# Eight places for the next pair's tokens, combined in product order; h loaded ahead of w_out

## The chip, the core and the metric

The kernel runs on one core of a Trainium2 chip. The engines of that core are PE (matrix multiplication, with PEld for its weight loads), DVE (vector operations), ACT (scalar operations and copies), POOL and SP. Each engine takes its instructions in the order of the program; SP issues the DMA transfers between the memory of the chip and the core's SBUF. The metric is the time of one execution on the device in microseconds (us), as a median over runs.

## The reference, cut

One layer of a decoder trunk on 4096 tokens of width 1024: an input projection to ten streams, five small mixers on them, a gate, an output projection and a layer norm.

```
def hybrid_mixer(x, mem, w_in, ...):
    proj = x @ w_in                                   # 4096 x 1024 @ 1024 x 3584
    xa, ba, ca, u, v, xc, da, dg, q, gate = jnp.split(proj, SPLIT_OFFSETS, axis=-1)
    ...
    y_d = conformer_conv(da, dg, cc_dw_w, ...)        # depthwise convolution, 31 taps
    ...
    h = jnp.concatenate([y_a, y_b, y_c, y_d, y_e], axis=-1) * jax.nn.silu(gate)
    return h @ w_out                                  # 4096 x 1280 @ 1280 x 1024

def reference(x, ...):
    y = hybrid_mixer(x, mem, ...)
    return layer_norm(DEEPNORM_ALPHA * x + y, ln_g[l], ln_b[l])
```

## The kernel before

**Input projection.** Tokens go in blocks of T = 512, and two blocks make a pair; there are four pairs. For each pair `mpair` runs 14 times. One `mpair` multiplies two groups of 128 output columns with the two blocks of the pair by a scheme of the Strassen kind: seven products (PA, PT1, PT2, PB, PT3, PD, PT4, in this order) in place of eight. Each factor of a product is an fp32 value split into a high and a low part, so that a product of four steps of 128 rows is 4 x 3 = 12 matmuls (L209, L211 and L212), and an `mpair` has 84. The sums over the products are made by DVE while it reads them from PSUM (`add`, L90: tiles t, v and three tiles cc). PSUM has four banks ("mm") for the products, so that a product late in an `mpair` needs a bank that DVE has read.

**Tokens.** The right factor of product i lies in four places of SBUF, x{i}{kap}h and x{i}{kap}l: kap 0 and 1 are the first and second half of its 512 rows, h and l the high and low part. `x_prep(p)` fills all 28 places of a pair: `load` (L134) brings a quarter block of 512 KB per half, eight in all, `step` combines quarters (`sub`, L93, in place, four times per half), and `put` splits the result into its places: a cast on ACT (L86) and a subtraction on DVE (L87, tile xl). The places are those of the pair before, so a place can be written when that pair's last `mpair` has run the product that reads it. For pairs 1 to 3 `x_prep` does half 0 with its four loads and seven steps, then half 1; all eight loads use the four buffers "raw", so those of half 1 wait for buffers that half 0 has done with. The call stands in front of the last `d_in` of the pair before.

**Weights.** Their splits are made in pair 0 and stored (wd); later pairs load them back (L202) in the order of use, through five buffers "ws".

**Between the products.** `d_conv` makes 60 steps of 1.28 us on DVE for the pair before (L462, tile acc, in a buffer "big" of five), spread over the first six `mpair`s of a pair; `d_tail` then has PE transpose the result (L428). `d_in` (L449, tile din, also "big") makes the input of that convolution.

**Output projection.** After the last pair all places x.. are reused. w_out is loaded in ten tiles (buffers "raw") and split into the first 20 places, ln_g and ln_b take two more, and the last six, from x51h on, take the first split tile of h, the gated mixer outputs (`load_h(0)`, three loads, tile hraw). Then 32 row tiles follow, each of 60 matmuls (L757): k from 0 to 9, and for each k two column halves with three matmuls each. The even row tiles take h from `load_h`.

The order of instructions on an engine is the order of the code; nothing reorders them but the tile framework's own scheduling, which fixes one order per engine when the program is built.

Of the kernel before, what the change touches and what calls it, by code (L numbers as in the profile page):

```python
# [11 lines left out]
F32 = mybir.dt.float32  # L12
# [15 lines left out]
NKO = DMIX // P  # L28
# [24 lines left out]
def trunk(ctx, tc, a, out):  # L53
    nc = tc.nc
# [9 lines left out]
    def nm(s):  # L64
        uid[0] += 1
        return f"{s}_{uid[0]}"
# [5 lines left out]
    def tt(tag, dt=F32, n=None):  # L72
        cols, bufs = SLOTS[tag]
        return tp.tile([P, cols], dt, tag=tag, name=nm(n or tag), bufs=bufs)
# [7 lines left out]
    def bank(pool, tag):  # L82
        return pool.tile([P, T], F32, tag=tag, name=nm(tag))

    def split_to(hi, lo, src):
        nc.scalar.copy(out=hi, in_=src)  # L86
        nc.vector.tensor_tensor(out=lo, in0=src, in1=hi.bitcast(F32), op=ALU.subtract)  # L87
# [4 lines left out]
    def sub(dst, x, y):  # L92
        nc.vector.tensor_tensor(out=dst, in0=x, in1=y, op=ALU.subtract)  # L93
# [24 lines left out]
    def x_place(i, kap):  # L118
        return [xc.tile([P, 2, T], F32R, tag=f"x{i}{kap}{s}", name=nm(f"x{s}")) for s in "hl"]

    def x_prep(p):

        xs = [[None, None] for _ in range(7)]
        raws = {}

        def put(i, kap, src):
            xs[i][kap] = x_place(i, kap)
            split_to(*xs[i][kap], src)

        def load(kap, j, n):  # L130
            tag = "big" if p == 0 and kap == 1 else "raw"
            raw = tt(tag, n="xraw")[:, :2 * T].rearrange("p (k t) -> p k t", k=2)
            k0 = 4 * j + 2 * kap
            nc.sync.dma_start(out=raw, in_=a["xT"][:, k0:k0 + 2, (2 * p + n) * T:(2 * p + n + 1) * T])  # L134
            raws[kap, j, n] = raw

        def step(kap, i):
            b11, b12, b22, b21 = (raws.get((kap, *q)) for q in ((0, 0), (0, 1), (1, 1), (1, 0)))
            if i == PT1:
                sub(b11, b12, b11)  # L140
            elif i == PT2:
                sub(b11, b22, b11)
            elif i == PT3:
                sub(b12, b22, b12)
            elif i == PT4:
                sub(b21, b21, b11)
            put(i, kap, {PA: b11, PT1: b11, PT2: b11, PB: b21, PT3: b12, PD: b22, PT4: b21}[i])

        if p == 0:
            for q in ((0, 0), (0, 1), (1, 1), (1, 0)):  # L150
                for kap in range(2):
                    load(kap, *q)
                yield
            for i in range(7):
                for kap in range(2):
                    step(kap, i)
                yield
        else:
            for kap in range(2):
                for q in ((0, 0), (0, 1), (1, 1), (1, 0)):  # L160
                    load(kap, *q)
                for i in range(7):
                    step(kap, i)
        yield xs

# [59 lines left out]
    def mpair(xs):  # L225


        def step(ps, x, start, stop):
            ready(1)
            product(ps, ahead.pop(0), x, start, stop)  # L230
            ready(5)

        A = bank(pm, "mm")
        step(A, xs[PA], True, False)
        t = tt("st", n="t")
        nc.scalar.copy(out=t, in_=A)  # L236
        C = bank(pm, "mm")
        step(C, xs[PT1], True, True)
        B = bank(pm, "mm")
        step(B, xs[PT2], True, True)  # L240
        add(t, B, t)
        v = tt("st", n="v")
        add(v, C, t)
        step(A, xs[PB], False, True)
        B2 = bank(pm, "mm")
        step(B2, xs[PT3], True, False)
        c22 = tt("cc", n="cc")
        add(c22, B2, v)
        C2 = bank(pm, "mm")
        step(C2, xs[PD], True, True)  # L250
        c12 = tt("cc", n="cc")
        add(c12, C2, v)
        step(B2, xs[PT4], False, True)
        c21 = tt("cc", n="cc")
        add(c21, B2, t)
        return (A, c12), (c21, c22)
# [13 lines left out]
    def begin(b, key, dst):  # L270
        if b == 0:
            nc.gpsimd.memset(dst, 0.0)
        else:
            nc.gpsimd.tensor_copy(out=dst, in_=halo[key])

    xg = x_prep(0)
    first = [{}, {}]

# [360 lines left out]
    def take(gen, count):  # L639
        for _ in range(count):  # L640
            if next(gen, "end") == "end":
                return
# [21 lines left out]
    for p in range(NPAIR):  # L664
# [15 lines left out]
        for i in range(2):  # L680
            q, ge = mpair(xs)
# [8 lines left out]
        if p < NPAIR - 1:  # L690
            xs = next(x_prep(p + 1))
# [5 lines left out]
    free = [xc_tag for i in range(7) for kap in range(2) for s in "hl" for xc_tag in (f"x{i}{kap}{s}",)]  # L697

    def place(dt=F32R, n="wo"):
        return xc.tile([P, 2 * T], dt, tag=free.pop(0), name=nm(n))  # L700

    wo = []
    for k in range(NKO):
        raw = tt("raw", n="woraw")
        nc.sync.dma_start(out=raw, in_=a["w_out"][k])
        wo.append((place(), place()))
        split_to(*wo[k], raw)
    lng, lnb = place(F32, "lng"), place(F32, "lnb")
    nc.sync.dma_start(out=lng, in_=a["ln_g"])
    nc.sync.dma_start(out=lnb, in_=a["ln_b"])  # L710
    htags = free[:6]

    def load_h(u):

        def part(j):
            if u % 2 == 0 or j == 4:
                return xc.tile([P, 2 * T], F32R, tag=htags[j if u % 2 == 0 else 5], name=nm("h"))
            return tt("ws", F32R, n="h")

        src = h[u // 2][:, u % 2]  # L720
        hs = [part(j).rearrange("p (k t) -> p k t", k=4) for j in range(5)]
        for j in range(3):
            n = 4 if j < 2 else 2
            raw = tt("raw", n="hraw").rearrange("p (k t) -> p k t", k=4)[:, :n]
            nc.sync.dma_start(out=raw, in_=src[:, 4 * j:4 * j + n])
            if j < 2:
                split_to(hs[j], hs[2 + j], raw)
            else:
                split_to(hs[4][:, :2], hs[4][:, 2:], raw)
        return [(hs[k // 4][:, k % 4], hs[2 + k // 4][:, k % 4]) if k < 8 else (hs[4][:, k - 8], hs[4][:, k - 6])  # L730
                for k in range(NKO)]

    hn = load_h(0)
    for b in range(NB):
        for c in range(NC4):
            r0 = b * T + c * P
            if c % 2 == 0:
                hh = hn
            elif r0 < SEQ - P:
                if r0 == (SEQ - 2 * T) - P:  # L740
                    take(conv, 60)
                    d_tail(NPAIR - 1, accs)
                hn = load_h((r0 + P) // 256)
            take(conv, 3)
            r = [tt("cc", n="r") for _ in range(2)]
            for n in range(2):
                nc.sync.dma_start(out=r[n], in_=a["x"][r0:r0 + P, T * n:T * n + T])
            st = sp.tile([P, 2, 6], F32, tag="st2", name=nm("st2"))
            ps = [bank(pm, "mm") for _ in range(2)]
            steps = [(n, k) for k in range(NKO) for n in range(2)]  # L750
            if r0 == SEQ - P:
                steps.sort()
            for n, k in steps:
                hi, lo = hh[k]
                whi, wlo = wo[k]
                for l, ww in ((lo, whi), (hi, wlo), (hi, whi)):
                    nc.tensor.matmul(out=ps[n], lhsT=l[:, P * (c % 2):P * (c % 2) + P], rhs=ww[:, T * n:T * n + T],  # L757
                                     start=(k == 0 and l is lo), stop=(k == NKO - 1 and ww is whi and l is hi))
            for n in range(2):
                nc.vector.scalar_tensor_tensor(out=r[n], in0=r[n], scalar=ALPHA, in1=ps[n],  # L760
                                               op0=ALU.mult, op1=ALU.add)
                nc.vector.bn_stats(out=st[:, n], in_=r[n])
            mv = sp.tile([P, 2], F32, tag="mv2", name=nm("mv2"))
            nc.vector.bn_aggr(out=mv, in_=st)
            rs = sp.tile([P, 1], F32, tag="rs2", name=nm("rs2"))
            rstd_of(rs, mv[:, 1:2], 1, EPS)
            for n in range(2):
                nc.vector.scalar_tensor_tensor(out=r[n], in0=r[n], scalar=mv[:, 0:1], in1=lng[:, T * n:T * n + T],
                                               op0=ALU.subtract, op1=ALU.mult)
                nc.vector.scalar_tensor_tensor(out=r[n], in0=r[n], scalar=rs, in1=lnb[:, T * n:T * n + T],  # L770
                                               op0=ALU.mult, op1=ALU.add)
                nc.sync.dma_start(out=out[r0:r0 + P, T * n:T * n + T], in_=r[n])
# [59 lines left out]
```

## Time and profile before

| | |
|---|---|
| median of 3 runs | 1802.05 us (1799.92 to 1803.36) |
| the profiled execution | 1802.25 us |
| its span in the trace | 1800.5 us |
| busy: PE, DVE, ACT, POOL | 97%, 74%, 28%, 2% |
| mean granted clock of TensorE | 0.992 |

The profiled execution takes 1.75 us more than its span; that part lies around the span. A busy PE of 97% leaves some 45 us in which PE did nothing. [...]

### The profile page before, as it was taken

The page shows a single profiled execution, that of the slowest core. Times are in us where ns is not written, and L with a number is a line of the kernel's source. Part 1 is how long each engine was busy: PE and PEld are TensorE (multiplying, and loading weights), DVE is VectorE, ACT ScalarE, POOL GpSimd, SP SyncE. Part 2 cuts the span into 40 slices and gives each one's busy share as a digit, 9 for nine tenths or more (in the row PEclk, how much of TensorE's full clock was granted, in tenths as well). Part 3 has the DMA queues.
Part 4 walks back from the last instruction along what each step waited for, and adds up shares of the span by engine and source line. Part 5 has one row for each costly group of instructions (what it writes and reads, how often), then busy time and mean ns, then how long its engine had stood idle before and what let it go on. Part 6 is the DMA issues. An engine that isn't in the chain of part 4 may idle for free.

```text
span 1800.5 us, 21764 instructions
## 1 busy us (share of the span) xinstructions
PE 1754.9 (97%) x7912; PEld 1383.6 (77%) x7912; DVE 1336.9 (74%) x2461; ACT 507.0 (28%) x937; POOL 44.8 (2%) x87
## 2 busy tenths in 40 slices
PE   5999999999999999999999999999989999999997
PEld 4887777878877787887778788777768888888786
DVE  8678887799966539997643999766379996665665
ACT  4323644420144423013532411354141010000300
POOL 0000000000100001010000000000000000000000
PEclk9999999999999999999999999999989999999999
DMA  7767455776744467675346766544683344332621
GB/s 276 274 239 261 183 198 196 280 238 208 235 163 137 133 217 270 201 230 177 129 151 211 269 201 213 197 143 141 205 289 99 119 132 141 127 100 79 213 71 47
DMA packets 128091, 332.79 MB, mean 185 GB/s; under 512 B 14064, under 2 KB 36080, under 8 KB 127984
## 3 DMA queue, kind: packets, MB, share of 16 engines
q1 hardware_dynamic: 127984, 331.39, 54.3%
q8 instruction: 63, 1.03, 0.2%
q14 instruction: 44, 0.36, 0.1%
HBM read 238.02 MB, written 93.32 MB: 184 GB/s over the span
## 4 chain that ended last, share of the span: by engine, by line
PE 91%; DVE 5%; DMA 2%; ACT 1%; issue 1%; SPq 0%; DVEq 0%; ACTq 0%
PE mm L757 24%; PE mm L209 19%; PE mm L212 19%; PE mm L211 19%; PE ax L632 3%; PE ax L607 2%; DVE xl L87 2%; PE ax L627 2%; DMA xraw<-in_xT 1%; DVE xraw L93 1%; PE ax L577 1%; PE ax L428 1%; PE ax L485 0%; PE ax L475 0%; PE ax L487 0%
## 5 line engine op out<-in xcount | busy, mean ns | idle before, releaser
L209 PE MATMUL mm<-xl,w 128*128 128x512 f32 x1568 | 627.4, 400 | 25.9 <-DVE xl L87 20.3
L211 PE MATMUL mm<-xh,w 128*128 128x512 f32 x1568 | 624.6, 398 | 0.9 <-DVE w L87 0.9
L212 PE MATMUL mm<-xh,w 128*128 128x512 f32 x1568 | 623.2, 398 | 0.0
L757 PE MATMUL mm<-wo,h 128*128 128x512 f32 x1920 | 445.8, 394 | 7.8 <-DVE h L87 7.8
L757 PEld LDWEIGHTS mm<-wo,h 128*128 128x128 f32 x1920 | 362.6, 189 | 87.6 <-DVE h L87 8.6
L209 PEld LDWEIGHTS mm<-xl,w 128*128 128x128 f32 x1568 | 297.1, 189 | 98.6 <-DVE xl L87 24.4
L212 PEld LDWEIGHTS mm<-xh,w 128*128 128x128 f32 x1568 | 296.8, 189 | 70.6 <-issue 3.6
L211 PEld LDWEIGHTS mm<-xh,w 128*128 128x128 f32 x1568 | 297.2, 190 | 68.2 <-issue 2.4
L462 DVE SCALAR_TENSOR_TENSOR acc<-din,c,acc 128x1024 f32<-128x1024 f32 x240 | 303.8, 1279 | 0.6 <-ACT acc L459 0.2
L86 ACT CAST h<-hraw 128x1024 fp32r<-128x1024 f32 (+1 forms) x48 | 43.3, 910 | 319.8 <-PE mm L757 235.3
L90 DVE TENSOR_TENSOR cc<-mm,v 128x512 f32<-128x512 f32 x112 | 76.8, 688 | 68.8 <-PE mm L212 68.3
L760 DVE SCALAR_TENSOR_TENSOR r<-r,mm 128x512 f32<-128x512 f32 x64 | 43.5, 687 | 79.8 <-PE mm L757 79.7
L86 ACT CAST xh<-xraw 128x1024 fp32r<-128x1024 f32 x56 | 57.9, 1051 | 64.2 <-DVE xraw L93 41.5
L90 DVE TENSOR_TENSOR t<-mm,t 128x512 f32<-128x512 f32 x56 | 38.6, 689 | 49.9 <-PE mm L212 49.9
L87 DVE TENSOR_TENSOR xl<-xraw,xh 128x1024 fp32r<-128x1024 f32 x56 | 66.7, 1221 | 11.3 <-ACT xh L86 11.1
L388 ACT ACTIVATE cc<-cc 128x512 f32<-128x512 f32 x44 | 27.9, 634 | 157.2 <-DVE cc L90 157.0
L87 DVE TENSOR_TENSOR h<-hraw,h 128x1024 fp32r<-128x1024 f32 (+1 forms) x48 | 49.7, 1041 | 26.3 <-issue 13.1
L236 ACT COPY t<-mm 128x512 f32<-128x512 f32 x56 | 32.9, 587 | 128.6 <-PE mm L212 128.5
L611 DVE TENSOR_REDUCE mx<-ax 128x2 f32<-128x512 f32 x64 | 42.7, 682 | 30.2 <-PE ax L607 29.9
L90 DVE TENSOR_TENSOR cc<-mm,t 128x512 f32<-128x512 f32 x56 | 38.5, 688 | 35.6 <-PE mm L212 35.1
L615 ACT ACTIVATE e<-ax,mx 128x256 f32<-128x256 f32 x128 | 59.3, 476 | 17.1 <-DVE mx L611 16.2
L435 ACT ACTIVATE nrm<-ax,nmr,rs 128x256 f32<-128x256 f32 x64 | 30.7, 570 | 115.9 <-DVE nmr L433 115.9
(147 smaller groups left out, 1531.8 us busy)
## 6 DMA issues: line engine op xcount, KB each, us to landing
w<-wd SPq DMA_DIRECT2D x294, 512.0 KB, 3.9
wd<-w SPq DMA_DIRECT2D x98, 512.0 KB, 2.9
xraw<-in_xT SPq DMA_DIRECT2D x32, 512.0 KB, 5.5
h<-cc SPq DMA_DIRECT2D x64, 256.0 KB, 3.1
hraw<-h SPq DMA_DIRECT2D x32, 512.0 KB, 4.1
r<-in_x SPq DMA_DIRECT2D x64, 256.0 KB, 3.0
out<-r SPq DMA_DIRECT2D x64, 256.0 KB, 2.0
wraw<-in_w_in SPq DMA_DIRECT2D x22, 512.0 KB, 4.3
```

What stands on the lines that cost most here:

```text
L86: nc.scalar.copy(out=hi, in_=src)
L87: nc.vector.tensor_tensor(out=lo, in0=src, in1=hi.bitcast(F32), op=ALU.subtract)
L90: nc.vector.tensor_tensor(out=dst, in0=x, in1=y, op=ALU.add)
L209: nc.tensor.matmul(out=ps, lhsT=w[:, 0, k], rhs=xl[:, r], start=start and k == 0, stop=False, skip_group_check=True)
L211: nc.tensor.matmul(out=ps, lhsT=w[:, 1, k], rhs=xh[:, r], start=False, stop=False, skip_group_check=True)
L212: nc.tensor.matmul(out=ps, lhsT=w[:, 0, k], rhs=xh[:, r], start=False, stop=stop and k == 3, skip_group_check=True)
L462: nc.vector.scalar_tensor_tensor(out=accs[i], in0=dins[i][:, k:k + 2 * T], scalar=dww[:, i, k:k + 1], in1=accs[i], op0=ALU.mult, op1=ALU.add)
L611: nc.vector.tensor_reduce(out=mx, in_=sc[j], axis=AX.X, op=ALU.max, negate=True)
L615: nc.scalar.activation(out=e[:, c], in_=sc[j][:, c], func=AF.Exp, bias=mx[:, c:c + 1], accum_out=su[:, c:c + 1])
L632: nc.tensor.matmul(out=po[64 * j:64 * j + 64], lhsT=vm[:, mc, 64 * hd:64 * hd + 64], rhs=pT, start=(mc == 0), stop=(mc == 1))
L757: nc.tensor.matmul(out=ps[n], lhsT=l[:, P * (c % 2):P * (c % 2) + P], rhs=ww[:, T * n:T * n + T], start=(k == 0 and l is lo), stop=(k == N ...
L760: nc.vector.scalar_tensor_tensor(out=r[n], in0=r[n], scalar=ALPHA, in1=ps[n], op0=ALU.mult, op1=ALU.add)
```

## The change

Two pieces of code are changed. In `x_prep` for pairs 1 to 3 the eight loads no longer share four buffers: half 0's four and the last of half 1 are in "raw", the other three of half 1 in "big". The eight are issued ahead of all steps, in the order in which the steps first use them, and the steps go product by product, both halves of product 0, both of product 1 and so on. In the output phase the six places for h are now the first six (x00h to x10l), `load_h(0)` stands ahead of w_out, whose ten tiles take the next 20 places (x11h to x60l), and ln_g and ln_b take x61h and x61l.

```diff
@@ -128,7 +128,7 @@
             split_to(*xs[i][kap], src)
 
         def load(kap, j, n):
-            tag = "big" if p == 0 and kap == 1 else "raw"
+            tag = "big" if kap == 1 and (p == 0 or (j, n) != (1, 0)) else "raw"
             raw = tt(tag, n="xraw")[:, :2 * T].rearrange("p (k t) -> p k t", k=2)
             k0 = 4 * j + 2 * kap
             nc.sync.dma_start(out=raw, in_=a["xT"][:, k0:k0 + 2, (2 * p + n) * T:(2 * p + n + 1) * T])
@@ -156,10 +156,11 @@
                     step(kap, i)
                 yield
         else:
-            for kap in range(2):
-                for q in ((0, 0), (0, 1), (1, 1), (1, 0)):
-                    load(kap, *q)
-                for i in range(7):
+            for kap, q in ((0, (0, 1)), (0, (0, 0)), (1, (0, 0)), (1, (0, 1)), (0, (1, 1)), (1, (1, 1)), (0, (1, 0)),
+                           (1, (1, 0))):
+                load(kap, *q)
+            for i in range(7):
+                for kap in range(2):
                     step(kap, i)
         yield xs
 
@@ -699,16 +700,7 @@
     def place(dt=F32R, n="wo"):
         return xc.tile([P, 2 * T], dt, tag=free.pop(0), name=nm(n))
 
-    wo = []
-    for k in range(NKO):
-        raw = tt("raw", n="woraw")
-        nc.sync.dma_start(out=raw, in_=a["w_out"][k])
-        wo.append((place(), place()))
-        split_to(*wo[k], raw)
-    lng, lnb = place(F32, "lng"), place(F32, "lnb")
-    nc.sync.dma_start(out=lng, in_=a["ln_g"])
-    nc.sync.dma_start(out=lnb, in_=a["ln_b"])
-    htags = free[:6]
+    htags = [free.pop(0) for _ in range(6)]
 
     def load_h(u):
 
@@ -731,6 +723,15 @@
                 for k in range(NKO)]
 
     hn = load_h(0)
+    wo = []
+    for k in range(NKO):
+        raw = tt("raw", n="woraw")
+        nc.sync.dma_start(out=raw, in_=a["w_out"][k])
+        wo.append((place(), place()))
+        split_to(*wo[k], raw)
+    lng, lnb = place(F32, "lng"), place(F32, "lnb")
+    nc.sync.dma_start(out=lng, in_=a["ln_g"])
+    nc.sync.dma_start(out=lnb, in_=a["ln_b"])
     for b in range(NB):
         for c in range(NC4):
             r0 = b * T + c * P
```

SP, from the second pair to the third, before: the rows are DMA issues in their order, w<-wd weights (wd_5_183 belongs to the second pair's last `mpair`, wd_0_87 and on to the third pair's first), xraw<-in_xT tokens. Ahead of these rows the loads 5814 to 5820 of half 0 were issued while the second pair's products ran.

```order
L202 DMA w_5713<-wd_5_183 128x1024
L202 DMA w_5730<-wd_6_184 128x1024
L202 DMA w_5745<-wd_0_87 128x1024
L202 DMA w_5762<-wd_1_88 128x1024
L134 DMA xraw_5854<-in_xT 128x2x512
L202 DMA w_5777<-wd_2_89 128x1024
L202 DMA w_5794<-wd_3_90 128x1024
L134 DMA xraw_5856<-in_xT 128x2x512
L202 DMA w_5810<-wd_4_91 128x1024
L134 DMA xraw_5858<-in_xT 128x2x512
L134 DMA xraw_5860<-in_xT 128x2x512
L202 DMA w_5916<-wd_5_92 128x1024
```

SP at the same place after the change. Here the loads 5814, 5816, 5822 and 5826 were issued ahead, as they use the "raw" buffers; 5828 is the eighth load.

```order
L203 DMA w_5687<-wd_4_182 128x1024
L134 DMA xraw_5818<-in_xT 128x2x512
L203 DMA w_5713<-wd_5_183 128x1024
L134 DMA xraw_5820<-in_xT 128x2x512
L203 DMA w_5730<-wd_6_184 128x1024
L134 DMA xraw_5824<-in_xT 128x2x512
L203 DMA w_5745<-wd_0_87 128x1024
L203 DMA w_5762<-wd_1_88 128x1024
L203 DMA w_5777<-wd_2_89 128x1024
L203 DMA w_5794<-wd_3_90 128x1024
L134 DMA xraw_5828<-in_xT 128x2x512
L203 DMA w_5810<-wd_4_91 128x1024
```

Three of the four late loads moved ahead of the third pair's first weight; one load, the eighth, stands in front of its fifth weight, where before the last three stood.

DVE at the same change of pairs, before: the rows that follow the last PSUM read of the second pair (cc_5812) and the two operations din_5894. L93 combines quarters, L87 writes a low part, L462 is a step of the convolution, and the last row is the first PSUM read of the third pair.

```order
L93 TENSOR_TENSOR xraw_5854<-xraw_5856,xraw_5854 128x1024
L462 SCALAR_TENSOR_TENSOR acc_6033<-din_5691,c_222,acc_6033 128x1024
L462 SCALAR_TENSOR_TENSOR acc_6439<-din_5894,c_222,acc_6439 128x1024
L87 TENSOR_TENSOR xl_5868<-xraw_5854,xh_5867 128x1024
L93 TENSOR_TENSOR xraw_5856<-xraw_5858,xraw_5856 128x1024
L93 TENSOR_TENSOR xraw_5854<-xraw_5858,xraw_5854 128x1024
L87 TENSOR_TENSOR xl_5877<-xraw_5860,xh_5876 128x1024
L87 TENSOR_TENSOR xl_5882<-xraw_5856,xh_5881 128x1024
L87 TENSOR_TENSOR xl_5873<-xraw_5854,xh_5872 128x1024
L87 TENSOR_TENSOR xl_5886<-xraw_5858,xh_5885 128x1024
L93 TENSOR_TENSOR xraw_5860<-xraw_5860,xraw_5854 128x1024
L90 TENSOR_TENSOR t_5918<-mm_5935,t_5918 128x512
```

DVE after the change, from the row behind cc_5812 on:

```order
L93 TENSOR_TENSOR xraw_5820<-xraw_5824,xraw_5820 128x1024
L87 TENSOR_TENSOR xl_5877<-xraw_5822,xh_5876 128x1024
L87 TENSOR_TENSOR xl_5881<-xraw_5824,xh_5880 128x1024
L87 TENSOR_TENSOR xl_5873<-xraw_5820,xh_5872 128x1024
L87 TENSOR_TENSOR xl_5863<-xraw_5828,xh_5862 128x1024
L93 TENSOR_TENSOR xraw_5826<-xraw_5826,xraw_5816 128x1024
L93 TENSOR_TENSOR xraw_5828<-xraw_5828,xraw_5818 128x1024
L450 SCALAR_TENSOR_TENSOR din_5894<-th_5895,cc_5812 128x512
L87 TENSOR_TENSOR xl_5886<-xraw_5826,xh_5885 128x1024
L450 SCALAR_TENSOR_TENSOR din_5894<-cc_5796,cc_5779 128x512
L87 TENSOR_TENSOR xl_5891<-xraw_5828,xh_5890 128x1024
L90 TENSOR_TENSOR t_5918<-mm_5935,t_5918 128x512
```

Before, nine rows of xraw and xl stood between cc_5812 and t_5918, with a tenth behind it; after, nine stand there and none behind. The two convolution steps that stood among them moved behind t_5918, and the two din operations came in.

ACT at the start of the output phase, before: L86 casts the high parts of wo (w_out) and h, L447 is the tanh of `d_in`, L459 the first tap of the convolution.

```order
L86 CAST wo_11215<-woraw_11213 128x1024
L86 CAST wo_11221<-woraw_11219 128x1024
L86 CAST wo_11227<-woraw_11225 128x1024
L447 ACTIVATE cc_11152<-cc_11152 128x512
L86 CAST wo_11233<-woraw_11231 128x1024
L459 ACTIVATE acc_11258<-din_11055,c_228,c_222 128x1024
L459 ACTIVATE acc_12385<-din_11168,c_228,c_222 128x1024
L86 CAST h_11241<-hraw_11246 128x1024
L86 CAST h_11242<-hraw_11250 128x1024
L86 CAST h_11245<-hraw_11254 128x512
```

ACT after the change, around the first h cast:

```order
L448 ACTIVATE cc_11037<-cc_11037 128x512
L86 CAST h_11178<-hraw_11186 128x1024
L86 CAST h_11177<-hraw_11182 128x1024
L237 COPY t_11079<-mm_11064 128x512
L86 CAST h_11181<-hraw_11190 128x512
L86 CAST wo_11196<-woraw_11194 128x1024
L86 CAST wo_11202<-woraw_11200 128x1024
L86 CAST wo_11208<-woraw_11206 128x1024
L448 ACTIVATE th_11169<-mm_11064 128x512
L86 CAST wo_11214<-woraw_11212 128x1024
```

The three casts of h moved from behind the last of the ten wo casts to ahead of the first.

## Rows read from the trace of the kernel before

**Rows 1.** Page, busy time of each engine: us (share of the span) xinstructions.
```profile
PE 1754.9 (97%) x7912; PEld 1383.6 (77%) x7912; DVE 1336.9 (74%) x2461; ACT 507.0 (28%) x937; POOL 44.8 (2%) x87
```

**Rows 2.** Waits of PE, whole span: who for, us in total, times, longest.
```profile
PE mm L209 <- DVE xl L87: 20.3, 9, 7.6
PE mm L757 <- DVE h L87: 7.8, 2, 6.7
PE mm L209 <- DVE t L90: 4.8, 3, 3.4
```

**Rows 3.** Waits of PE in the first 45 us of the program.
```profile
PE mm L209 <- DVE xl L87: 13.3, 5, 7.6
PE mm L209 <- DVE t L90: 3.4, 1, 3.4
```

**Rows 4.** Windows, L209 only: us, PE and PEld busy (x), PEclk, DMA share, GB/s.
```profile
335.84:355.44 19.60, 11.06 (x28) 5.26 (x28) 1.00 0.78 265
355.44:381.29 25.85, 11.88 (x29) 5.64 (x28) 0.93 0.73 244
662.85:682.37 19.52, 11.05 (x28) 5.28 (x28) 1.00 0.63 214
682.37:704.92 22.55, 11.48 (x29) 5.26 (x28) 1.00 0.79 272
986.58:1006.10 19.52, 11.05 (x29) 5.28 (x28) 1.00 0.63 212
1006.10:1028.32 22.22, 11.36 (x28) 5.27 (x28) 1.00 0.79 283
1290.44:1309.96 19.52, 11.05 (x28) 5.27 (x28) 1.00 0.74 240
1309.96:1337.46 27.50, 11.14 (x28) 5.09 (x27) 0.92 0.84 297
```

**Rows 5.** Windows, L757 only: the first and second row tile of the output phase.
```profile
1337.46:1354.06 16.60, 16.59 (x61) 13.42 (x61) 0.82 0.77 256
1354.06:1367.66 13.60, 13.60 (x61) 11.27 (x60) 1.00 0.12 39
```

**Rows 6.** Windows, all of PE: the two stretches at half clock.
```profile
370.80:374.10 3.30, 3.30 (x10) 0.50 0.61 209
1333.40:1343.50 10.10, 6.04 (x14) 0.50 0.87 287
```

**Rows 7.** Chain of waits from 348 to 372 us: start, us, what.
```profile
356.05 5.56 DMA xraw<-in_xT
```

**Rows 8.** Tile xraw: ns min/median/max of its casts, subtractions and landings.
```profile
L86 ACT CAST xh<-xraw x56: 1036/1052/1059, 5.3 to 1021.9; 128x1024 fp32r<-128x1024 f32 x56
L87 DVE TENSOR_TENSOR xl<-xraw,xh x56: 1212/1222/1226, 6.3 to 1023.5; 128x1024 fp32r<-128x1024 f32 x56
...
DMA to landing us min/median/max: 3.6/5.5/9.0
```

**Rows 9.** Timeline of DVE at the second change of pairs.
```profile
683.92 0.68 DVE L90 TENSOR_TENSOR cc<-mm,t 128x512 f32<-128x512 f32 x1
...
692.67 4.62 DVE L87 TENSOR_TENSOR xl<-xraw,xh 128x1024 fp32r<-128x1024 f32 x4
...
698.35 0.69 DVE L90 TENSOR_TENSOR t<-mm,t 128x512 f32<-128x512 f32 x1
```

**Rows 10.** Windows, all of DVE: first and second change to the convolution's end.
```profile
682.37:818.01 135.64, 132.10 (x148) 1.00 0.71 233
355.44:496.17 140.73, 134.88 (x151) 0.99 0.70 231
```

**Rows 11.** Timeline of DVE and PE where the first convolution ends.
```profile
494.89 1.28 DVE L462 SCALAR_TENSOR_TENSOR acc<-din,c,acc 128x1024 f32<-128x1024 f32 x1
...
497.01 0.49 PE L428 MATMUL ax<-c,acc 128*128 128x128 f32 x3
```

**Rows 12.** Waits of SP, whole span.
```profile
SPq L134 <- DVE xl L87: 5.1, 5, 2.4
```

## The prediction

> **What bounds the kernel now.** I began with the busy times: PE does something in 97% of the span, DVE in 74% [rows 1], so PE is the bound and time can come only from the some 45 us in which it stands or runs slowly. The waits of PE say who it stood for: the low parts of the tokens (xl) 20.3 us in nine waits, the first h of the output phase 7.8 us in two, the PSUM reads of tile t 4.8 us in three [rows 2]. The start of the program holds 13.3 us of the first and 3.4 of the third [rows 3]; x_prep(0) and the first weights are not touched, so this part stays. What is left sits where the tokens of a pair give way to the next pair's, and where the output phase begins.
>
> To price these four places I read windows that hold one whole `mpair` each, the last of a pair and what follows it. Each holds 28 matmuls of L209, a third of the 84 [rows 4]. An undisturbed `mpair` takes 19.52 us, 2.79 us a product. The first `mpair` of the second pair takes 25.85 (6.25 over the 19.60 of the one before it), of the third 22.55 (3.03 over), of the fourth 22.22 (2.70 over). The last `mpair` of the fourth pair, with the wait for h that follows it, takes 27.50 (7.98 over). The first row tile of the output phase takes 16.60 us at a mean granted clock of 0.82, the second 13.60 at 1.00, so 3.00 over [rows 5]. The five excesses add up to **22.96 us**, the most that this change can give back.
>
> The clock's share lies inside that sum. PEclk was 0.50 in 370.8 to 374.1 us, after the long waits of the first change of pairs, and in 1333.4 to 1343.5 us, after the wait for h [rows 6]. Ten matmuls took 3.30 us in the first, against 10 x 0.232 = 2.32 at full clock (19.52/84 each); the second holds the slow half of the first row tile. At the second and third change the granted clock stayed at 1.00 [rows 4].
>
> **The change, part by part.** *Tokens.* Before, half 1's loads waited until half 0's splits gave back their buffers. At the first change the chain of waits runs through such a load: it took 5.56 us, and PE waited behind it [rows 7]. After the change seven loads are issued before the pair ends (the order of SP shows it), and the bytes and operations are the same: 14 casts of 1.052 us on ACT, 14 subtractions and 8 combinations of 1.222 us on DVE per pair [rows 8], 22 x 1.222 = 26.9 us of DVE. Each place still comes free as its product ends in the old pair and is needed six products later, 16.7 us on. So DVE cannot have everything done before the change: it gets free places faster (one product in 2.79 us) than it fills them (22 x 1.222/7 = 3.8 us). What matters is the order in which it catches up, and product order is the order of need.
>
> I follow the queue of DVE at a change of pairs. Let S be the time at which the new pair should start. The last PSUM read of the old pair begins at 683.92 and lasts 0.68, thus ends at S + 2.23 with S = 682.37 [rows 9, 4]. Behind it the order of DVE shows nine token operations and two din before the next read, of t. Four token operations in a row took 4.62 us [rows 9], 1.155 each; a din, half as wide, is put at the 0.68 of the cc read. That is 10.4 + 1.4 us, so t begins at S + 14.0 and ends at S + 14.7. PE wants the bank that t frees for PD, after five products, at S + 13.95: a wait of **0.7 us** at each change, 2.1 in all. Before, t began at 698.35, S + 16.0, as two convolution steps of 1.28 stood ahead of it; they have moved behind. The low part needed most urgently is PB's half 1, fifth in that queue: done at S + 2.23 + 5 x 1.155 = S + 8.0, and needed at three and a half products, S + 9.8.
>
> *The eighth load* waits for the "raw" buffer of the quarter that PT3's half 0 read; that subtraction stands two before the last PSUM read and ends near S + 0.4. With the median landing of 5.5 us [rows 8] and a cast it is ready at S + 6.95, as DVE comes to it at S + 6.9. I cost it at nothing; the price of a late landing is a rival below.
>
> *Buffers "big".* The convolution's accumulators take buffers that tokens now hold until near S + 10, so its 60 steps begin later and must still end before PE reaches their transposes. DVE was busy 134.88 of 140.73 us from the first change to the convolution's end, 132.10 of 135.64 from the second [rows 10]. At the first change the last step ended 0.84 us before PE began the transposes at 497.01 [rows 11]. With the stall taken out, PE comes there at 497.01 - 6.25 + 0.7 + 0.23 (one matmul more ahead of it in the order of PE), S + 136.25 with S = 355.44. DVE has one token operation fewer there: 133.7 busy, and with the 3.5 us of idle time of the second change it ends at S + 137.2. That is a wait of some **0.9 us**. At the other two changes the transposes stand nine matmuls (2.1 us) later than before, which covers a stall shortened by less than 2.7; I cost them at nothing.
>
> *Output phase.* The h tile's places come free with PA and PT1 of the last `mpair`, not with PD and PT4, and its loads are issued a whole pair ahead. Nothing then keeps PE from the first row tile but the last reads of PSUM, some 0.3 us by their spacing. w_out follows: k = 0 is needed at once and each further k 1.36 us later (13.60/10) [rows 5], k = 9 after 12.2 us. Its place is PT4's half 0; after that product ends, a cast and a subtraction need 2.3 us, so some 10 us cover it, and the ten splits of 1.22 us on DVE begin 16.7 us before the phase. DVE's total work is the same here too. With no wait the clock has no reason in the rows to fall, so the 3.00 us of the first row tile go as well.
>
> **The sum.** 22.96 - 2.1 - 0.9 - 0.3 = 19.7 us. From the profiled execution's 1802.25 us that gives **1782.6 us**; the median of the runs shown, 1802.05, stands 0.2 below it, too little to matter.
>
> *The clock by another road.* Without the start, xl leaves 20.3 - 13.3 = 7.0 us of waits, t 4.8 - 3.4 = 1.4, and the longest wait for h was 6.7 [rows 2, 3]: 15.1 us. The half clock adds 0.98 (3.30 - 2.32) and 3.00, so 19.1 of the 22.96 are named, and the rest are short gaps between. [...]
>
> **The rivals.** *DVE falls behind (0.12).* If each token operation takes its whole 1.222 us with one cast of 1.052 uncovered, t ends at S + 2.23 + 11.0 + 1.4 + 0.7 + 1.05 = S + 16.4, 2.4 us late at each change, 7.2 in place of 2.1: **1787.7 us**. For it: DVE has no idle time in these stretches. Against it: the measured 4.62 for four.
>
> *The convolution ends later (0.10).* If DVE finishes no sooner after the first change than before, at S + 140.73 [rows 10], PE waits 4.5 us there instead of 0.9: **1786.2 us**. For it: the later start of the accumulators.
>
> *The eighth load lands late (0.08).* At the longest landing, 9.0 us [rows 8], its low part is done at S + 11.7, PE waits 1.9 us for PB, the queue of DVE slips by 3.7 us and t costs PE 2.5 more; 4.4 per change instead of 0.7, so +11.1: **1793.7 us**. It rests on DVE taking its queue strictly in order. [...]
>
> *The clock still falls (0.03).* Waits of 0.7 us would have to do what the second and third change, with 3.03 and 2.70 us over, did not: +3.98, **1786.6 us**.
>
> *Slower than before (0.03).* SP also takes its queue in order, and the eighth load stands ahead of the new pair's fifth weight. Weights go out four products ahead, 11.2 us; with a landing like the tokens' 5.5, some 5.7 us are to spare. If SP stood there longer, each further us would cost PE one at each of three changes. It decides at 5.7 + 19.7/3 = 12.3 us: a block of 14 us would cost 24.9, and **1807.5 us** result. The longest such wait of SP was 2.4 us [rows 12].
>
> *Nothing changes (0.04).* Loads come no earlier, since another buffer binds: **1802 us**. Against it: the order of SP.
>
> My forecast has 0.60. The range of **1777 to 1794 us** takes in the first four rivals above, and at its lower end all 22.96 us with the some 2 us by which runs differ. It leaves out 0.07 above. A measurement of this kernel tells some 0.2% (3.6 us) from no change: faster 0.93, the same 0.04, slower 0.03.
>
> **What would show it right or wrong.** In the new profile the three `mpair`s after a change of pairs should take 19.5 to 20.5 us, the waits for xl should be those of the start alone, the wait for h should be gone and the granted clock should be 1.00 from 50 us on. PE should wait for t about 0.7 us at each change and about 1 us at L428 once. A wait of PE for xl at a change would mean a late eighth load; a DVE-bound t above 2 us would mean that the queue was mispriced; a weight w late would mean SP. If the first row tile still takes 16 us, the clock has another cause than the wait.

## The result and the profile after

The changed kernel takes 1783.79 us (median of 4 runs, 1783.38 to 1784.19) against 1802.68 for the kernel before in the same job: a ratio of 0.9898 (95% interval 0.9881 to 0.9915), which is 18.4 us of 1802.68; the two medians differ by 18.9. In a second job on another occasion it took 1781.54 (1780.40 to 1781.91) against 1802.17: 0.9883 (0.9870 to 0.9897). The forecast was 1782.6. The profiled execution took 1783.74 us, with a span of 1782.0.

The page's busy times, which answer to [rows 1]:

```profile
PE 1749.8 (98%) x7912; PEld 1380.8 (77%) x7912; DVE 1333.9 (75%) x2461; ACT 504.4 (28%) x937; POOL 45.6 (3%) x87
```

PE's waits over the whole span, which answer to [rows 2]:

```profile
PE mm L210 <- DVE xl L87: 13.5, 5, 7.6
PE mm L210 <- DVE t L90: 5.1, 2, 4.1
PE mm L758 <- DVE h L87: 1.3, 1, 1.3
```

Of xl's 13.5 us all lie in the first 45 us, as do 4.1 of t's 5.1. The waits for xl at the three changes of pairs are gone, and so is the long wait for h; the 1.3 us left belong to a later row tile.

Windows with the matmuls of L210 (L209 before): the first two `mpair`s of the program, then the first two of the second, third and fourth pair, then the last of the fourth. The columns are those of [rows 4]; PEclk is the clock granted to PE as a share of the full one, 1.00:

```profile
7.56:80.24 72.68, 25.30 (x56) 11.98 (x57) 0.93 0.74 268
356.52:396.82 40.30, 22.21 (x56) 10.53 (x56) 1.00 0.77 257
678.60:717.64 39.04, 22.09 (x56) 10.56 (x56) 1.00 0.73 255
999.62:1038.82 39.20, 22.12 (x57) 10.51 (x56) 1.00 0.73 247
1301.52:1321.62 20.10, 11.16 (x28) 5.09 (x27) 1.00 0.76 265
```

Two undisturbed `mpair`s take 2 x 19.52 = 39.04 us. The second pair's first two are 1.26 over, the third's nothing, the fourth's 0.16. (They are read in twos because the mark between the two falls 0.23 us earlier in the changed kernel than in the one before.) Before they were 45.37, 42.07 and 41.74 with the second `mpair` at 19.52 [rows 4], so the changes of pairs gave back 5.07, 3.03 and 2.54 us. The last `mpair` of the fourth pair takes 20.10 where it took 27.50.

The first and second row tile of the output phase, which answer to [rows 5]:

```profile
1321.62:1335.26 13.64, 13.64 (x60) 11.26 (x60) 1.00 0.97 352
1335.26:1348.87 13.61, 13.61 (x62) 11.26 (x60) 1.00 0.67 223
```

Both run at the full clock; the first gave back 2.96 us. DVE at the second change of pairs, which answers to [rows 9]:

```profile
679.19 0.69 DVE L90 TENSOR_TENSOR cc<-mm,t 128x512 f32<-128x512 f32 x1
...
680.92 4.63 DVE L87 TENSOR_TENSOR xl<-xraw,xh 128x1024 fp32r<-128x1024 f32 x4
...
691.20 0.69 DVE L90 TENSOR_TENSOR t<-mm,t 128x512 f32<-128x512 f32 x1
```

The last read of the old pair ends at 679.88, 1.28 us after the new pair's start at 678.60, and t ends at 691.89, S + 13.29. PE comes to its bank at 692.54, S + 13.94, and finds it free. The end of the first convolution, which answers to [rows 11]:

```profile
491.19 1.28 DVE L463 SCALAR_TENSOR_TENSOR acc<-din,c,acc 128x1024 f32<-128x1024 f32 x1
...
493.25 0.60 PE L429 MATMUL ax<-c,acc 128*128 128x128 f32 x4
```

The last step ends at 492.47 (S + 135.95), and PE comes to the transposes 0.78 us later without a wait.

### The profile page after: what moved, and what is told of

Its sections match the earlier page's. It is cut to its first block, busy times and chain, and to the rows that moved or that the text cites. A ratio compares the mean times of both kernels' runs of the same rounds, so it can differ in the third digit from the quotient of the medians.

```text
span 1782.0 us, 21763 instructions
## 1 busy us (share of the span) xinstructions
PE 1749.8 (98%) x7912; PEld 1380.8 (77%) x7912; DVE 1333.9 (75%) x2461; ACT 504.4 (28%) x937; POOL 45.6 (3%) x87
## 4 chain that ended last, share of the span: by engine, by line
PE 94%; DVE 3%; DMA 2%; ACT 1%; issue 0%; SPq 0%; DVEq 0%; ACTq 0%
PE mm L758 24%; PE mm L213 20%; PE mm L210 20%; PE mm L212 20%; PE ax L633 3%; PE ax L608 2%; PE ax L628 2%; DVE xl L87 1%; PE ax L578 1%; PE ax L429 1%; DMA xraw<-in_xT 1%; DVE xraw L93 1%; PE ax L486 0%; PE ax L476 0%; PE ax L488 0%
## 5 line engine op out<-in xcount | busy, mean ns | idle before, releaser
L210 PE MATMUL mm<-xl,w 128*128 128x512 f32 x1568 | 625.6, 399 | 18.8 <-DVE xl L87 13.5
L210 PEld LDWEIGHTS mm<-xl,w 128*128 128x128 f32 x1568 | 296.5, 189 | 88.8 <-DVE xl L87 15.5
L86 ACT CAST h<-hraw 128x1024 fp32r<-128x1024 f32 (+1 forms) x48 | 43.4, 909 | 311.9 <-PE mm L758 224.0
L87 DVE TENSOR_TENSOR xl<-xraw,xh 128x1024 fp32r<-128x1024 f32 x56 | 66.4, 1221 | 6.7 <-ACT xh L86 6.7
L86 ACT CAST xh<-xraw 128x1024 fp32r<-128x1024 f32 x56 | 56.9, 1047 | 46.5 <-DVE xraw L93 24.0
L87 DVE TENSOR_TENSOR h<-hraw,h 128x1024 fp32r<-128x1024 f32 (+1 forms) x48 | 50.2, 1047 | 23.3 <-ACT h L86 12.9
L633 PE MATMUL ax<-pT,c 128*64 128x512 f32 x128 | 58.9, 617 | 0.8
```

Of the source, the lines that this page charges most:

```text
L210: nc.tensor.matmul(out=ps, lhsT=w[:, 0, k], rhs=xl[:, r], start=start and k == 0, stop=False, skip_group_check=True)
L633: nc.tensor.matmul(out=po[64 * j:64 * j + 64], lhsT=vm[:, mc, 64 * hd:64 * hd + 64], rhs=pT, start=(mc == 0), stop=(mc == 1))
```

## The experiments

Each of these kernels was timed beside the kernel before. Twelve profiles beside that of before show that the first two `mpair`s of the program, which no kernel here touches, took from 70.0 to 72.7 us; differences of a microsecond between kernels are therefore read in windows, not in medians.

**The two parts apart.** Tokens alone (the x_prep part of the diff):

> Only the tokens of the change: eight places and product order; the output phase is that of before. Theory: the two parts act in different places and add up. The changed kernel gave back 5.06, 3.02 and 2.55 us at the three changes of pairs, so 10.6 us here and some 1792 us; the wait for h of 6.7 us and the slow first row tile (16.6 us) stay. Rival: part of the gain at the output phase came from tokens being ready earlier or from DVE being less late there; then this one gains more than 12 us and the other part alone less than 9.

Measured: 1791.80 us, ratio 0.9941 (0.9922 to 0.9960), 10.0 less than before. PE's waits where its output phase begins:

```profile
PE mm L758 <- DVE h L87: 6.7, 1, 6.7
```

The wait is that of before, and the first row tile took 16.20 us. The first `mpair` after each change of pairs, in this kernel and then in the changed one:

```profile
354.66:375.48 20.82, 11.17 (x28) 5.26 (x28) 1.00 0.90 311
677.51:696.80 19.29, 11.05 (x28) 5.29 (x28) 1.00 0.91 320
998.56:1017.93 19.37, 11.06 (x28) 5.26 (x28) 1.00 0.89 318
```

```profile
356.52:377.07 20.55, 11.17 (x28) 5.25 (x28) 1.00 0.89 312
678.60:697.89 19.29, 11.04 (x28) 5.28 (x28) 1.00 0.90 322
999.62:1018.99 19.37, 11.06 (x29) 5.26 (x28) 1.00 0.87 306
```

The changes of pairs are as in the changed kernel.

The output phase alone (the second and third part of the diff):

> Only the output phase of the change: h in the first six places and loaded ahead of w_out; the tokens are those of before. Theory: 7.41 + 2.95 = 10.4 us less than before, some 1792.3 us, with the three changes of pairs as before (6.2, 3.0 and 2.7 us over an undisturbed block). Rival, as for the tokens alone: less than 9 us. Beside it: in the one profile of the changed kernel the first two blocks of the program took 1.2 us longer than in the one of before. If that comes from the change of tokens it is absent here; if it is spread between executions it may show here too.

Measured: 1795.15 us (1789.66 to 1796.79), ratio 0.9953 (0.9936 to 0.9970), 6.6 less. Its first two `mpair`s after each change of pairs:

```profile
355.58:401.71 46.13, 23.11 (x56) 10.94 (x56) 0.96 0.73 244
683.55:725.55 42.00, 22.49 (x56) 10.56 (x56) 1.00 0.77 263
1007.33:1051.29 43.96, 22.65 (x57) 10.55 (x56) 1.00 0.71 252
```

Over 39.04 these are 7.09, 2.96 and 4.92 us. The last `mpair` and the first row tile (19.53 and 13.64 us) gave back all 10.9 us, but in this execution, which is the median one, the first and third change cost 3.0 us more than in the profile of before. So the parts act in separate places, as expected. The 6.6 us lie below the 9 at which the rival begins, but its other half, more than 12 us for the tokens alone, did not come (10.0), and the windows show where the rest went: to a worse draw at changes that are still open to late loads. The start of this execution took 71.3 us, so the long start of the changed kernel's first profile (72.7) isn't read from it either way; the later runs settle it as spread.

**Is it the order or the buffers?** The half order, on the changed kernel:

```diff
-            for i in range(7):
-                for kap in range(2):
+            for kap in range(2):
+                for i in range(7):
                     step(kap, i)
```

> The changed kernel with its eight places and early loads, but the steps half by half again: seven steps of half 0, then seven of half 1. Theory as the prediction put it (what matters is the order in which DVE catches up): half 1's low parts are late again, PE waits 1 to 1.5 us for xl at each change, 1787 to 1788 us. Rival: early loads are all that mattered, since the order on DVE is nearly the same for either (eight token operations and two din between the last read of a pair and t, nine before); then 1783.8 us, within 1 us, or a little less because t comes earlier.

Measured: 1781.32 us (1780.07 to 1782.71), ratio 0.9883 (0.9862 to 0.9903); no wait of PE for xl at any change. Then the one line on the buffers alone, with the loads in the old order too (output phase as changed):

```diff
-            tag = "big" if p == 0 and kap == 1 else "raw"
+            tag = "big" if kap == 1 and (p == 0 or (j, n) != (1, 0)) else "raw"
```

> The changed kernel with one line of the token part alone: the choice of buffers. The loads and the steps are in the old order again, four loads and seven steps of half 0, then of half 1. Theory after the run with the half order: the four more buffers are the whole of the token part, because the order in which DVE gets the operations is made by the scheduler from what is ready; 1781 to 1783 us, no slower than the changed kernel. Rival: the order of the loads matters, half 1's first quarters land later and PE waits for xl at each change; 1786 us or more.

> The changed kernel as it is, on the same chip as the next three, to compare with. 1783.8 us within 1 us. The first two blocks of the program took 71.5 us before, 72.7 after, and 71.0, 71.3, 72.3 and 71.0 in four other profiles; if that is spread between executions, this one lies anywhere in 70.9 to 72.8.

Measured in one job: 1781.62 us (0.9885, 0.9872 to 0.9899) and, for the changed kernel again, 1781.54. The one line's `mpair`s in twos after each change:

```profile
354.49:393.75 39.26, 22.07 (x56) 10.53 (x56) 1.00 0.75 255
676.19:715.23 39.04, 21.93 (x56) 10.55 (x56) 1.00 0.71 247
997.19:1036.39 39.20, 21.96 (x57) 10.51 (x56) 1.00 0.71 235
```

0.22, nothing and 0.16 us over (with the half order 39.27, 39.03 and 39.20 us in all): no worse than with the product order, and 0.4 to 1.0 us better at the first change. The rival of the first expectation and the theory of the second hold, and my theory of the order is refuted. The order of DVE, as the program was built, shows why: at the second and third change ten rows stand between the last read of the old pair and t in both kernels, eight of them token operations, where the changed kernel has eleven and nine. So turning the loops round moved one operation. That the tile framework puts operations in the order in which it reckons they are ready is my reading; the runs show only the orders that it built. What these two kernels win at the first change they lose in the eighth `mpair` of that pair, where PE waits to transpose a tile of another mixer, which it does not in the changed kernel:

```profile
PE ax L428 <- DVE v L404: 1.0, 1, 1.0
```

The changed kernel again came out 2.3 us below its first job, more than the 1 us expected: in its profile the first two `mpair`s took 1.3 us less, the first change 0.65, and one late row tile 0.95.

**How many buffers.** Half the dose, on the kernel with the one line: two quarters in "big", two in "raw".

```diff
-            tag = "big" if kap == 1 and (p == 0 or (j, n) != (1, 0)) else "raw"
+            tag = "big" if kap == 1 and (p == 0 or j == 0) else "raw"
```

> Half the dose: the choice of buffers alone, with two of half 1's quarters in big and two in raw, so six of the eight loads need not wait. Theory (early loads are the whole of the token part): the two late quarters are needed by the third product at the earliest; the three changes give back part of their 10.6 us, 1783 to 1788 us. Rival (each late load stalls as before, since DVE takes its queue in order): as if none were early, 1791 to 1795 us as with the output part alone.

Measured: 1782.18 us (1781.04 to 1785.97), ratio 0.9891 (0.9875 to 0.9907). The first two `mpair`s of the program, then those after each change:

```profile
8.03:78.05 70.02, 25.10 (x57) 11.73 (x57) 0.93 0.76 276
354.16:393.48 39.32, 22.05 (x56) 10.51 (x56) 1.00 0.76 266
676.54:715.62 39.08, 21.94 (x56) 10.54 (x56) 1.00 0.78 258
997.45:1036.49 39.04, 21.93 (x57) 10.55 (x56) 1.00 0.73 249
```

0.28, 0.04 and nothing over: as good as three in "big", better than my theory's 1783 to 1788. Six loads that need not wait are enough. The other way, on the changed kernel, all four of half 1 in "big":

```diff
-            tag = "big" if kap == 1 and (p == 0 or (j, n) != (1, 0)) else "raw"
+            tag = "big" if kap == 1 else "raw"
```

> The changed kernel with the eighth load too in a buffer big, so that it needs no raw buffer to be given back. Theory (the eighth load costs nothing, as predicted): the order of DVE ahead of t holds the same nine token operations less one, t 1.2 us earlier; at most the 0.9 us of the first change come back, 1782.9 to 1783.8 us. Rival: with four tokens and two din on five big buffers the second din waits, the convolution starts later and PE waits at its transposes: above 1785 us.

Measured: 1782.65 us (1781.82 to 1783.56), ratio 0.9891 (0.9877 to 0.9904), beside 1781.54 for the changed kernel in that job. Its windows were 1.24, 0.16 and 0.16 over. At the second and third change the eighth load was issued 7.3 us earlier than in the changed kernel and nothing was gained, so there its wait for a buffer costs nothing. At the first change it was issued no earlier (0.56 us behind the new pair's start, 0.61 in the changed kernel), landed at S + 6.26 and kept DVE idle for 0.37 us. PE did not wait at the convolution's transposes, so the second din doesn't pay for the buffer.

**The queue of DVE ahead of t.** Two token operations more in each of pairs 1 to 3 (PD's low parts are written twice):

```diff
             split_to(*xs[i][kap], src)
+            if p and i == PD:
+                hi, lo = xs[i][kap]
+                sub(lo, src, hi.bitcast(F32))
```

> The changed kernel with two token operations more on DVE for each pair from the second on: the low parts for PD are written twice with the same values. Theory (the queue of DVE ahead of t is what binds next; in the profile t ended 0.7 us ahead of PE's need at the second change and 0.9 us late at the first): t ends 2.3 us later, so PE waits 1.6 us more at two changes and 2.3 at the first, 5.5 us in all, and the convolution may end late on top: 1787 to 1790 us beside 1781.5 to 1783.8. Rival: DVE has slack enough, within 1 us of the changed kernel.

Measured: 1788.75 us (1787.90 to 1790.23), ratio 0.9924 (0.9912 to 0.9935). The first `mpair` after each change, and PE's wait at the first:

```profile
354.45:379.44 24.99, 11.85 (x28) 5.55 (x28) 0.93 0.75 259
680.69:701.75 21.06, 11.16 (x28) 5.28 (x28) 1.00 0.86 288
1003.50:1024.55 21.05, 11.18 (x28) 5.25 (x28) 1.00 0.81 280
```

```profile
PE mm L213 <- DVE t L90: 3.6, 1, 3.6
```

The second and third change took 21.06 and 21.05 us where the changed kernel has 19.29 and 19.37: 1.7 each for 2.3 us more of DVE, as the 0.65 us of slack that t had demand. The first, with the `mpair` behind it (44.51 us for the two), took 4.2 us more than the changed kernel's 40.30, more than the expected 2.3: DVE also stood idle for 0.95 us until the eighth load had landed (S + 6.75) and was cast, and the granted clock was 0.93, since with a wait of 3.6 us in one piece the half clock came back there.

Two operations fewer on DVE, by giving the last combination of each half to POOL:

```diff
             elif i == PT4:
-                sub(b21, b21, b11)
+                (nc.gpsimd if p else nc.vector).tensor_tensor(out=b21, in0=b21, in1=b11, op=ALU.subtract)
```

> The changed kernel with the last combination of each half (for PT4, two per pair from the second pair on) on POOL instead of DVE. Theory: what is left at the first change is DVE's queue ahead of t (1.2 us over), so two operations of 1.15 us less let t end 2.3 us earlier, the wait of 0.9 us goes, and the time is 1782.8 us. Rival: POOL takes several us for one, DVE's low parts of PT4 stand ahead of t in its queue and wait for it, and t comes later: each us of POOL beyond the some 6 us that the queue leaves costs up to 1 us at each of three changes, so 1785 to 1795 us.

Measured: 1792.55 us (1789.13 to 1795.45), ratio 0.9944 (0.9923 to 0.9964); 9 to 11 us worse than the changed kernel's two medians. The tile xraw there:

```profile
L87 DVE TENSOR_TENSOR xl<-xraw,xh x56: 1209/1222/3424, 6.3 to 1019.8; 128x1024 fp32r<-128x1024 f32 x56
...
L146 POOL TENSOR_TENSOR xraw<-xraw,xraw x6: 2403/3312/6672, 359.4 to 1012.0; 128x1024 f32<-128x1024 f32 x6
```

POOL took a median of 3.31 us for what DVE does in 1.22, and a subtraction of DVE's took up to 3.42 us in place of 1.22, as long as POOL's. At the second and third change DVE stood idle for 3.4 us until POOL's result, which had taken 6.67, was cast, and t came late. This is the rival, and the price is on both sides.

**The output phase.** h in the early places, but loaded behind w_out (`hn = load_h(0)` moved below ln_b):

> The changed kernel with h in the first six places as there, but loaded behind w_out as before. Theory: the wait for h came from its loads and casts standing behind w_out's in the queues of SP, ACT and DVE; 4 to 7 us of wait come back and with them the low clock in the first row tile (3 us): 1791 to 1794 us. Rival: the late places (free only after the last two products) were the cause, and the order of loads is worth nothing: 1783.8 us within 1.

Measured: 1789.19 us (1787.18 to 1791.68), ratio 0.9928 (0.9915 to 0.9942). PE's wait, and the first two row tiles:

```profile
PE mm L758 <- DVE h L87: 6.1, 1, 6.1
```

```profile
1324.82:1340.94 16.12, 16.12 (x60) 13.12 (x61) 0.84 0.92 341
1340.94:1354.50 13.56, 13.56 (x61) 11.25 (x60) 1.00 0.21 69
```

The wait is back, and the low clock with it (16.12 against 13.56 us). The median lies under the expected range, but 7.7 us above the changed kernel of that job; the two tiles with the `mpair` ahead of them (25.75) took 55.43 us. The other half, h loaded first but in the late places (`htags = free[22:28]`):

> The changed kernel with h loaded first as there, but in the last six places as before (free only as the last two products end). Theory: loads and order were the wait, and the places cost little: the three splits of h need 1.05 + 1.22 us each after the last product, some 3 us behind its end; 1785 us, and a first row tile at full clock since the wait is below that of 6 us. Rival: the late places alone bring the wait back, 6 us and the low clock with 2.5 to 3 us: 1790 us.

Measured: 1783.43 us (1783.11 to 1783.96), ratio 0.9894 (0.9880 to 0.9908). Its first two row tiles:

```profile
1319.50:1334.47 14.97, 14.42 (x60) 11.09 (x61) 1.00 0.93 303
1334.47:1348.44 13.97, 13.91 (x61) 11.19 (x60) 1.00 0.94 333
```

Here PE waited 0.7 us for h and 0.4 for wo, the clock stayed at 1.00, and the two tiles with the `mpair` ahead of them (20.35) took 49.29 us against 47.35 in the changed kernel (20.10 + 13.64 + 13.61). So the order of the loads is worth some 8 of the output's 10 us (55.43 - 47.35) and the places some 2 (49.29 - 47.35).

## Why the prediction was right, and where it was not

**The excesses** [rows 4, 5] were the right quantity, and they are where the gain is: 5.07 + 3.03 + 2.54 at the changes of pairs and 27.50 + 16.60 - 20.10 - 13.64 = 10.36 at the output, 21.0 of 22.96 us. Tokens alone and the output alone each gave back their own places.

**The wait for t**, put at 0.7 us a change, was 0.9 at the first and none at the others. The queue behind the last read was as long as counted (t ended 12.01 us after that read, predicted 12.5), but the read ended at S + 1.28, not S + 2.23: its place before was itself behind late token work. Two operations more cost 1.7 us each at the second and third change, which fits a slack of 0.65 us (13.94 - 13.29), so this is what binds next.

**The first change** kept 1.26 us where 0.7 was forecast; in the second profile of the changed kernel it was 39.65, 0.61 over. I had counted the rows of the second change for all three. DVE at the first:

```profile
357.68 1.22 DVE L87 TENSOR_TENSOR xl<-xraw,xh 128x1024 fp32r<-128x1024 f32 x1
359.45 5.77 DVE L87 TENSOR_TENSOR xl<-xraw,xh 128x1024 fp32r<-128x1024 f32 x5 [0.55 <-ACT xh L86]
...
370.88 0.68 DVE L90 TENSOR_TENSOR t<-mm,t 128x512 f32<-128x512 f32 x1
```

Ten token operations stand ahead of t there, not nine, and an idle 0.55 us for a load that landed 1.83 us behind the new pair's start; t ends at S + 15.04. In the second profile the idle time is gone and t ends at S + 14.4; with the half order, nine operations, it ends at S + 13.9 and nothing is left to wait for. The late load was the seventh. The eighth, which I had priced, landed at S + 5.62 in time, but in two of the other kernels it was late there, and DVE stood idle for 0.37 and 0.95 us. Its price rested on DVE taking its queue in order: in the trace of the changed kernel the eleven rows of DVE between the old pair's last read and t at the second change stand in the order as built.

**Product order as the order that matters** is the step that failed. The prediction said that what matters is the order in which DVE catches up; the half order and the old loads did as well in windows and medians (the order moved 0.4 to 1.0 us at the first change, and some 0.8 the other way later in that pair). What matters is that the loads are not held back by four buffers, and six that are free already do it. The forecast came out since the built order on DVE, from which I counted, was right, whatever wrote it.

**The convolution's end**, 0.9 us in the sum, cost nothing. I had DVE busy 133.7 us with 3.5 idle. The window to PE's arrival, with the columns of [rows 10], shows less work in it, three instructions fewer than before, where I had counted one:

```profile
356.52:493.25 136.73, 132.55 (x148) 1.00 0.72 231
```

The step ended at S + 135.95, 1.25 us ahead of the forecast, and PE came at S + 136.73 rather than S + 136.25. The term was mis-sized by the 0.9 us.

**Output and clock** came as forecast: 0.62 us were left (20.10 - 19.52 and 13.64 - 13.60) where 0.3 was predicted, and the first row tile ran at full clock. The clock's own share was misread in the prediction. PE in the kernel before, at the first change:

```profile
370.66 0.55 PE L209 MATMUL mm<-xl,w 128*128 128x512 f32 x1
...
374.31 0.40 PE L209 MATMUL mm<-xl,w 128*128 128x512 f32 x1
```

Nine matmuls begin from the first of these rows to just ahead of the last; they took 3.65 us, against 9 x 0.232 = 2.09. The window of 3.30 us had counted ten because it counts those that it cuts at its edges. So the half clock cost 1.56 us there, not 0.98, and 19.7 of the 22.96 are named, not 19.1; the price of the rival in which the clock still falls was too low by the same 0.6. The sum does not change, since the windows hold the clock's share however it is counted.

**What the sum lacked.** The sum gave back 19.7 us and the places 21.0; the profiled executions differ by 18.5. The first two `mpair`s took 72.68 us against 71.46 before, and a later row tile 0.3 more. In the rest of the pairs, from the third `mpair` to the next change, the marks of the windows lie 281.78, 281.98 and 262.70 us apart, against 281.56, 281.66 and 262.12 before: 1.1 us more. 21.0 - 1.2 - 0.3 - 1.1 = 18.4. The first is spread (70.0 to 72.7 us in thirteen profiles of an unchanged stretch); what makes the 1.1 us was not tested. The forecast came within 1.2 us in part by luck: 1.3 us more given back than summed, and 2.6 lost elsewhere.

None of the kernels tried beats the changed kernel beyond that spread. The one line on the buffers with the output part is its equal.

## What to carry to other kernels

Where loads for the next stage share a few buffers with work that ends late, count the buffers before the order: two more gave all of the tokens' share here, and a loop turned round gave nothing on balance, since the built order of the engine, which decides, hardly changed. Price a boundary by whole windows over an undisturbed one rather than by the named waits (22.96 against 19.7 us here), and then ask how much slack the next wait in line has (0.65 us here). A transfer that will be needed first belongs ahead in the issuing queue, even where its place comes free late: here the order of the loads was worth some 8 of the output's 10 us.

## What the runs showed of the hardware

In the run with POOL a subtraction of DVE's that began at 360.36, while one of POOL's ran from 359.39 to 362.70, took 3.42 us in place of 1.22, beside POOL's 3.31. Another of POOL's took 6.67 us, while four subtractions of DVE's took 1.21 us each. What slowed them was not shown.

The granted clock fell to 0.50 after single waits of 3.6, 6.1 and 6.7 us, and at the first change of the kernel before after 4.2 us in two pieces, the longer of 2.9. It stayed at 1.00 after 0.9 and 1.5 us, after 0.7 and 0.4 in two pieces, and where the kernel before lost 3.03 us with 1.5 and 0.7 in two. In the run with POOL it fell at the first change (waits of 1.9 and 1.1 us) and at the second (2.3 in one piece), with a mean of 0.93 over the `mpair` at each, and stayed at 1.00 at the third after 2.2 in one piece.
